# Wide weight blocks of an MLP: the last activation group transposed half a unit earlier, and one wide block made plain

## The chip, the cores and the metric

One core of a Trainium2 chip runs the whole kernel. TensorE multiplies, VectorE (DVE) and ScalarE (ACT) prepare operands and drain results, SyncE (SP) and GpSimd (POOL) issue DMAs. The metric is the device time of one execution in microseconds.

## The reference

A two-layer decoder trunk over 256 tokens of width 2048, in float32. Each layer has a mixer (a recurrent one, then attention) and an MLP with 8192 hidden features. The change is in the MLP:

```python
def squared_relu_mlp(h, w1, w2):
    return jnp.square(jax.nn.relu(h @ w1)) @ w2

h = h + squared_relu_mlp(rms_norm(h, norm_mlp[layer]), mlp_w1[layer], mlp_w2[layer])
```

## The kernel before

**Three products for one.** Each float32 operand is split into a high part (the value rounded by a cast on ACT) and a low part (what is left, a subtraction on DVE). A product is then hi x hi, lo x hi and hi x lo. In the trace the weight tiles are named `hi` and `lo`. Activations and their low parts lie side by side in `bufa` (the MLP's input) and `bufb` (the hidden features: four tiles of four feature blocks each).

**Seven products for eight.** The MLP runs in four quarters of 2048 hidden features. A quarter multiplies by w1 (2048 x 2048) and then by w2 (2048 x 2048), each as two matrices of two 512-column halves (`first`, `second`, called with n = 0 and n = 2). `blocks` (line 896) computes one such matrix. For some pairs of 128-row feature blocks it uses seven products in place of eight: two token halves, two feature blocks and two column halves make a 2 x 2 by 2 x 2 product, done with sums of the operands. Sums of activations lie in `formx` and `formh`; sums of weights are made by DVE (`s<-raw,t`, then `s<-s,raw`) and by accumulating DMAs on POOL. The units t1, a, t2, c, t3, d, t4 hold the seven products of four pairs, 12 matmuls each. The remaining rows are multiplied plainly, in units called n with 24 matmuls, 12 for each token half. A plain matrix has four n units: 7 x 12 + 4 x 24 = 180 matmuls.

**Wide blocks.** The second w1 matrix of each quarter (`wider`, line 112) uses two pairs more: two of the n units are replaced by e1 to e4 (42 matmuls for 48). Their weight sums are made from half-size pieces (`make_more`, line 228), and the activation sums that they need (`more_forms`, line 869) are made once per layer, by entries of `steps` that are run one entry per unit (line 974). The host lays out the rows of w1 for this (`by_rows`, line 1425).

**What orders the work.** `ORDERS` (line 1367) gives the order of units. Each unit fetches the weights of a unit two places ahead: SP issues the load, ACT casts to `hi`, DVE subtracts to `lo`. There are three buffers each for raw, hi and lo weights, so a cast waits until TensorE has done with the unit three places back. TensorE's order is fixed by the code, since each matmul is chained to the one before. On ACT and DVE a scheduler orders by priority, and `after` adds order without a wait. Every engine takes its instructions strictly in that order.

**Turning the hidden features.** When both token halves of a hidden column group are done, `to_h` (line 977) puts a piece of work into `later`: eight transposes by TensorE into two banks `pl`, two casts by ACT into `bufb` and two subtractions by DVE for the low parts (called the bufb lows below). `flush` runs such pieces, at the end of an n unit (line 970). In the second w1 matrix the last group but one to be turned is group 3, whose work is flushed in unit n3, just ahead of the last unit t4. Its casts come after the latest weight cast (`casts`). A later weight's low part comes after the bufb lows (`turned_h`, line 213).

Line 68 is where DVE and ACT instructions are issued, line 300 the matmuls, line 303 the transposes.

Of the kernel before, what the change touches and what calls it, by code (L numbers as in the profile page):

```python
# [41 lines left out]
def trunk_kernel(ctx, tc, head, x, xtok, xback, cols, tab, masks, pos, fin, w_in, w_gate, w_out, w_qkv, w_o, w1, w2, out):  # L42
# [66 lines left out]
    def plan(src, n):  # L109
        units.extend((src, i) for i in range(n))  # L110

    wider = lambda src, i: src is w1 and i % 16 == 8
    order_of = lambda src, i: ORDERS[3 if wider(src, i) else 0 if src is w1 and i not in (0, 64) or src is w_o and not i
                                     else 2 if src is w2 and i == 120 else 1]

# [65 lines left out]

    held = {}
    turned_h = []

    def combine(u, src, i, what, i0):
        def load(name, j, home=wraw):
            held[name] = home.tile([P, 2048], F32, name="raw" if home is wraw else "bufb2" if home is act else name)
            nc.sync.dma_start(held[name], src[j])

        def add(to, x, y):  # L190
            return V.tensor_tensor(held[to], held[x], held[y], OP.add)

        if what == "t1":
            load("t1", i, both)
            load("a", i0)
            held["s"] = both.tile([P, 2048], F32, name="s")
            i = add("s", "a", "t1")
            if src is w_qkv and i0 == 8:
                after(i, [made[u - 1].ins.name])
        elif what in ("n", "d", "e2"):  # L200
            load(what, i)
        elif what == "e1":
            load("e1", i, act)
        def make(step=2048):
            if what[0] == "e":
                make_more(u, src, what, i0)
                return
            made[u] = Weights(held[{"t1": "s", "t2": "s", "t3": "t1", "t4": "s"}.get(what, what)], step)

        if what == "n" and src is w2 and i0 % 16 == 0 and i == i0 + 6:  # L210
            make()
            for name in turned_h:
                tc.add_manual_dep(made[u].ins, name, NOSYNC, reason="order on one engine")
            return
        ahead = units[u + 1][2:3] if u + 1 < len(units) else ()
        if ahead == ("t2",):
            load("c", i0 + 5)
            nc.gpsimd.dma_start(held["t1"], src[i0 + 5], accum_op=OP.add)
            if (src is w2 and (i0 == LATE_SUM or i0 % 16 == 0)) or (src is w1 and i0 == 64):
                make()  # L220
                after(add("s", "s", "c"), [made[u].ins.name])
                return
            add("s", "s", "c")
        make()
        if what == "c":
            nc.gpsimd.dma_start(held["s"], src[i0 + 1], accum_op=OP.add)
# [80 lines left out]
    def flush(due=None):  # L307
        todo = later[:due]
        del later[:due]
        for f in todo:  # L310
            f()
# [8 lines left out]
    def after(ins, names):  # L320
        ins = getattr(ins, "ins", ins)
        for n in names:
            tc.add_manual_dep(ins, n, NOSYNC, reason="order on one engine")
        return ins.name
# [571 lines left out]
    def blocks(src, i0, n0, mov, forms, events, final):  # L896
# [47 lines left out]
        for m, (what, u) in enumerate(order):  # L944
            w = unit(src, None if u is None else i0 + 4 * n0 + u)
            due = len(later)
            if what in extra:
                for bank_, at, get in extra[what]:
                    times(bank_, w, get, at, terms=2)
            elif what == "t4" and src is w2 and i0 + 4 * n0 == 120:  # L950
                times(beta, w, side[what], 0, S, beta[:, :S])
                final(0, 1, beta)
                rest = psc.tile([P, 512], F32, name="pt", bufs=1)
                times(rest, w, side[what], S, S, rest[:, :S])
                events["rest"](rest[:, :S])
            elif what != "n":
                times(bank[what], w, side[what])
                if what == "a":
                    seed(gamma, beta)
                elif what == "t1":  # L960
                    seed(delta, alpha)
                elif what in events:
                    events[what](bank[what])
            else:
                n, g = divmod(u, 4)
                for j in range(2):
                    times(sums[n, j], w, lambda i, j=j, g=g: plain(j, 4 * g + i))
                    if ends[n, j] == m:
                        final(n, j, sums[n, j])
                flush(due)  # L970
            if what in ("c", "e2", "t4", "e4") and (what, src, i0 + 4 * n0) != ("t4", w2, 120):
                finish_sums(m)
            turn_some()
            for f in steps.pop(0) if steps else ():
                f()

    def to_h(n, tiles):
        def work():
            ps = []
            turned_h.clear()  # L980
            for y in tiles:
                ps.append(psc.tile([P, 4, P], F32, name="pl", bufs=2))
                for i in range(4):
                    turn(ps[-1][:, i], y[:, i * P:i * P + P])
            with urgent():
                for j, p in enumerate(ps):
                    b = bufb[:, 4 * n:4 * n + 4]
                    if n < 2 and j:
                        b, p = b[:, 1::2], p[:, 1::2]
                    h = b[..., j * P:j * P + P]  # L990
                    after(A.copy(h, p), casts if n == 3 else ())
                    turned_h.append(after(V.tensor_tensor(b[..., S + j * P:S + j * P + P], p, h.bitcast(F32), OP.subtract), []))
                if n < 2:
                    z = tiles[1].rearrange("p (k c) -> p k c", k=4)
                    A.copy(z, ps[1])
                    t = tiles[0].rearrange("p (k c) -> p k c", k=4)
                    (s2, s4), (a21, a22), (a11, a12) = (
                        [v.rearrange("p (m two) c -> p two m c", two=2)[:, e] for e in range(2)] for v in (t, z, ps[0]))
                    combos(a22, s2, a21, s4, a11, a21, a12, a22)
                    for v, at in ((z, slice(1, 4, 2)), (t, slice(0, 4, 2))):  # L1000
                        part_forms(formh, 2 * n, 2, at, v.rearrange("p (m two) c -> p m two c", two=2))
        later.append(work)
# [76 lines left out]
    def mlp(layer, nrm, nxt, gname):  # L1079
# [10 lines left out]
        V.tensor_scalar(r2n, r2, -1.0, None, op0=OP.mult)  # L1090
        if not gname:
            after(lut(spare, epsc, AF.Abs_reciprocal_sqrt), casts)
        steps[:] = [[] for _ in range(5)] + [[lambda: more_forms(0)], [], [lambda: more_forms(1)]]
        for q in range(4):
            ends = nxt if q == 3 else None

# [303 lines left out]
def _layout(a):  # L1400
# [27 lines left out]
        t[10], t[14] = (both[:, :, k::2].reshape(P, 4, 512) for k in range(2))  # L1428
        return t.reshape(16, P, 2048)

    w1 = np.concatenate([by_rows(toks(n(w)[:, q * 2048:q * 2048 + 2048], PAIRED)) for w in a["mlp_w1"] for q in range(4)])
    w2 = np.concatenate([toks(n(w)[q * 2048:q * 2048 + 2048], PAIRED) for w in a["mlp_w2"] for q in range(4)])
    xs = n(a["x"]).reshape(2, P, D)
    xback = xs[1, ::-1]
# [35 lines left out]
```

## Time and profile before

| | |
|---|---|
| median of 3 runs | 2108.83 us (2107.88 to 2110.83) |
| profiled execution, its own time | 2113.02 us |
| its span, first to last instruction | 2111.2 us |
| granted TensorE clock, mean | 0.999 |
| read from HBM | 506.94 MB, 241 GB/s over the span |

The span is the time between the first and the last instruction; the execution's own time holds in addition what lies before and after. Busy time of TensorE counts a matmul from its start to its modelled end, and matmuls overlap: they start every 0.227 us while one is given 0.39 us. So a start that is late by less than the overlap shows up as busy time, and lateness is read better from the distance between the starts of two places in the program. In the names of the trace `out<-in` is what an instruction writes and reads, without the numbers of buffers; `p`, `pd`, `po` and `pt` are accumulators.

### The profile page before, as it was taken

The page shows a single profiled execution, that of the slowest core. Times are in us where ns is not written, and L with a number is a line of the kernel's source. Part 1 is how long each engine was busy: PE and PEld are TensorE (multiplying, and loading weights), DVE is VectorE, ACT ScalarE, POOL GpSimd, SP SyncE. Part 2 cuts the span into 40 slices and gives each one's busy share as a digit, 9 for nine tenths or more (in the row PEclk, how much of TensorE's full clock was granted, in tenths as well). Part 3 has the DMA queues.
Part 4 walks back from the last instruction along what each step waited for, and adds up shares of the span by engine and source line. Part 5 has one row for each costly group of instructions (what it writes and reads, how often), then busy time and mean ns, then how long its engine had stood idle before and what let it go on. Part 6 is the DMA issues. An engine that isn't in the chain of part 4 may idle for free.

```text
span 2111.2 us, 24900 instructions
## 1 busy us (share of the span) xinstructions
PE 2096.7 (99%) x9652; PEld 1738.3 (82%) x9652; DVE 1769.4 (84%) x1695; ACT 1395.6 (66%) x1530; POOL 87.8 (4%) x107
## 2 busy tenths in 40 slices
PE   9999999999999999999999999999999999999998
PEld 8888888877888888888888888888888888888886
DVE  7686978988888888888988788799888887988887
ACT  7577556676576567567666777677756755765765
POOL 0000000000000000000000000000000000000000
PEclk9999999999999999999999999999999999999999
DMA  8544557878878888888888777778788789788785
GB/s 346 181 162 158 180 202 217 289 215 251 270 230 281 276 240 253 283 248 230 280 248 251 212 215 233 217 239 260 234 268 277 229 252 310 235 247 276 231 288 162
DMA packets 73047, 510.67 MB, mean 242 GB/s; under 512 B 8160, under 2 KB 8544, under 8 KB 12896
## 3 DMA queue, kind: packets, MB, share of 16 engines
q1 hardware_dynamic: 58320, 413.38, 51.8%
q0 software_dynamic: 14464, 95.43, 24.7%
q8 instruction: 76, 1.25, 0.2%
q14 instruction: 43, 0.35, 0.0%
q10 hardware_dynamic: 144, 0.26, 0.0%
HBM read 506.94 MB, written 2.10 MB: 241 GB/s over the span
## 4 chain that ended last, share of the span: by engine, by line
PE 83%; DVE 8%; issue 3%; DMA 3%; ACT 2%; SPq 0%; DVEq 0%; ACTq 0%
PE p L300 53%; PE pd L300 12%; PE po L300 11%; DVE lo L68 5%; PE pt L300 3%; ACT hi L68 2%; DMA raw<-in_w 2%; DVE s L68 2%; PE pl L303 2%; PE pl L300 2%; DVE bufb L68 1%; DMA raw<-in_w_in 1%; DVE y L68 0%; DMA both_in<-in_head 0%; DVE formx L68 0%
## 5 line engine op out<-in xcount | busy, mean ns | idle before, releaser
L68 DVE TENSOR_TENSOR lo<-raw,hi 128x2048 fp32r<-128x2048 f32 (+2 forms) x357 | 767.3, 2157 | 134.8 <-ACT hi L68 133.7
L68 ACT CAST hi<-raw 128x2048 fp32r<-128x2048 f32 (+2 forms) x357 | 641.6, 1807 | 230.9 <-PE p L300 120.6
L300 PE MATMUL p<-hi,bufa 128*128 128x512 f32 x1872 | 474.6, 393 | 0.0
L300 PEld LDWEIGHTS p<-hi,bufa 128*128 128x128 f32 x1872 | 348.1, 188 | 69.7
L68 DVE TENSOR_TENSOR lo<-s,hi 128x2048 fp32r<-128x2048 f32 x123 | 281.6, 2290 | 103.2 <-ACT hi L68 102.9
L68 ACT CAST hi<-s 128x2048 fp32r<-128x2048 f32 x123 | 235.2, 1912 | 197.8 <-DVE s L68 163.3
L300 PE MATMUL p<-hi,bufb 128*128 128x512 f32 x1240 | 310.1, 391 | 0.0
L300 PEld LDWEIGHTS p<-hi,bufb 128*128 128x128 f32 x1240 | 231.7, 188 | 48.1 <-DVE bufb L68 0.2
L300 PE MATMUL p<-lo,bufa 128*128 128x512 f32 x936 | 255.3, 390 | 0.1
L300 PEld LDWEIGHTS p<-lo,bufa 128*128 128x128 f32 x936 | 175.7, 188 | 37.7 <-DVE lo L68 1.0
L300 PE MATMUL p<-lo,bufb 128*128 128x512 f32 x620 | 169.2, 392 | 1.9 <-DVE lo L68 1.3
L300 PEld LDWEIGHTS p<-lo,bufb 128*128 128x128 f32 x620 | 115.6, 188 | 29.9 <-DVE lo L68 6.3
L68 DVE TENSOR_TENSOR s<-s,raw 128x2048 f32<-128x2048 f32 x41 | 93.8, 2287 | 6.3 <-DMA raw<-in_w_qkv 3.2
L68 DVE TENSOR_TENSOR lo<-t,hi 128x2048 fp32r<-128x2048 f32 x41 | 93.7, 2286 | 3.0 <-ACT hi L68 3.0
L68 DVE TENSOR_TENSOR s<-raw,t 128x2048 f32<-128x2048 f32 x41 | 93.8, 2287 | 0.2
L300 PE MATMUL p<-hi,formx 128*128 128x512 f32 x368 | 92.1, 392 | 0.2 <-DVE formx L68 0.2
L68 ACT CAST hi<-t 128x2048 fp32r<-128x2048 f32 x41 | 78.6, 1918 | 17.5 <-PE po L300 6.8
L300 PE MATMUL pd<-hi,bufa 128*128 128x512 f32 x352 | 88.2, 393 | 0.0
L300 PE MATMUL po<-hi,bufb 128*128 128x512 f32 (+1 forms) x352 | 88.0, 387 | 0.0
L300 PEld LDWEIGHTS p<-hi,formx 128*128 128x128 f32 x368 | 68.4, 188 | 14.8 <-DVE formx L68 0.7
L300 PE MATMUL po<-hi,bufa 128*128 128x512 f32 x296 | 77.5, 393 | 1.0 <-ACT y L68 1.0
L300 PEld LDWEIGHTS po<-hi,bufb 128*128 128x128 f32 x352 | 65.7, 188 | 13.5
(328 smaller groups left out, 2723.0 us busy)
## 6 DMA issues: line engine op xcount, KB each, us to landing
raw<-in_w SPq DMA_DIRECT2D x216, 1024.0 KB, 6.8
raw<-in_w_in SPq DMA_DIRECT2D x45, 1024.0 KB, 4.8
raw<-in_w_qkv SPq DMA_DIRECT2D x42, 1024.0 KB, 5.2
t<-in_w SPq DMA_DIRECT2D x32, 1024.0 KB, 7.7
t<-in_w POOLq DMA_DIRECT2D x32, 1024.0 KB, 9.0
s<-in_w POOLq DMA_DIRECT2D x32, 1024.0 KB, 9.3
raw<-in_w_out SPq DMA_DIRECT2D x15, 1024.0 KB, 4.8
raw<-in_w_o SPq DMA_DIRECT2D x14, 1024.0 KB, 5.1
```

The source lines that it names most:

```text
L68: i = call(*args, **kw)
L300: chain[:] = [after(T.matmul(*args, **kw), chain)]
L303: chain[:] = [after(T.transpose(out_, in_, ident), chain)]
```

## The change

1. Unit n3 of a wide block flushes the turning of group 3 after its first 12 matmuls instead of after all 24.
2. In `to_h` the casts of group 3 no longer follow the latest weight cast, and its low parts follow the latest first sum `s<-raw,t` (`first_sum`).
3. The second w1 matrix of layer 0's first quarter is no longer wide: it takes the plain order of four pairs, and its w1 rows keep the plain layout. In layer 0 `more_forms` runs 24 units into the MLP, in the first w2 matrix, instead of 5.

```diff
-    wider = lambda src, i: src is w1 and i % 16 == 8
+    wider = lambda src, i: src is w1 and i % 16 == 8 and i != 8
...
+    first_sum = []
...
             i = add("s", "a", "t1")
+            first_sum[:] = [after(i, [])]
             if src is w_qkv and i0 == 8:
...
                     if ends[n, j] == m:
                         final(n, j, sums[n, j])
+                    if not j and not n and wider(src, i0 + 4 * n0):
+                        flush(due)
+                        due = 0
                 flush(due)
...
                     h = b[..., j * P:j * P + P]
-                    after(A.copy(h, p), casts if n == 3 else ())
-                    turned_h.append(after(V.tensor_tensor(b[..., S + j * P:S + j * P + P], p, h.bitcast(F32), OP.subtract), []))
+                    A.copy(h, p)
+                    turned_h.append(after(V.tensor_tensor(b[..., S + j * P:S + j * P + P], p, h.bitcast(F32), OP.subtract), first_sum if n == 3 else []))
...
-        steps[:] = [[] for _ in range(5)] + [[lambda: more_forms(0)], [], [lambda: more_forms(1)]]
+        steps[:] = [[] for _ in range(5 if layer else 24)] + [[lambda: more_forms(0)], [], [lambda: more_forms(1)]]
...
-    w1 = np.concatenate([by_rows(toks(n(w)[:, q * 2048:q * 2048 + 2048], PAIRED)) for w in a["mlp_w1"] for q in range(4)])
+    w1 = [toks(n(w)[:, q * 2048:q * 2048 + 2048], PAIRED) for w in a["mlp_w1"] for q in range(4)]
+    w1 = np.concatenate(w1[:1] + [by_rows(w) for w in w1[1:]])
```

How this moves instructions, at three places. TensorE at the end of the wide block in layer 0's third quarter, before (unit n3 in the first four rows, the transposes of group 3, then t4):

```order
L300 MATMUL p<-hi,bufa 128x512 x8
L300 MATMUL p<-lo,bufa 128x512 x4
L300 MATMUL po<-hi,bufa 128x512 x8
L300 MATMUL po<-lo,bufa 128x512 x4
L303 MATMUL pl<-tab__188,y_6073 128x128 x4
L303 MATMUL pl<-tab__188,y_6013 128x128 x4
L300 MATMUL po<-hi,bufa 128x512 x8
L300 MATMUL po<-lo,bufa 128x512 x4
```

The same place now:

```order
L302 MATMUL p<-hi,bufa 128x512 x8
L302 MATMUL p<-lo,bufa 128x512 x4
L305 MATMUL pl<-tab__188,y_6061 128x128 x4
L305 MATMUL pl<-tab__188,y_6001 128x128 x4
L302 MATMUL po<-hi,bufa 128x512 x8
L302 MATMUL po<-lo,bufa 128x512 x4
L302 MATMUL po<-hi,bufa 128x512 x8
L302 MATMUL po<-lo,bufa 128x512 x4
```

The eight transposes stand 12 matmuls sooner. DVE at the same place, before (`s<-raw,t` is the first sum of the w2 matrix that follows, `bufb_2514<-pl` the bufb lows of group 3):

```order
L68 TENSOR_TENSOR s<-raw,t_6159 128x2048
L68 TENSOR_TENSOR lo<-s,hi 128x2048
L68 TENSOR_TENSOR bufb_2514<-pl,bufb_2514 128x4x128 x2
L68 TENSOR_TENSOR lo<-raw,hi 128x2048 x2
L68 TENSOR_TENSOR s<-s,raw 128x2048
```

DVE there now:

```order
L68 TENSOR_TENSOR s<-raw,t_6147 128x2048
L68 TENSOR_TENSOR bufb_2514<-pl,bufb_2514 128x4x128 x2
L68 TENSOR_TENSOR lo<-s,hi 128x2048
L68 TENSOR_TENSOR lo<-raw,hi 128x2048 x2
L68 TENSOR_TENSOR s<-s,raw 128x2048
```

The lows stand between the sum and its low part; the same holds in all seven wide blocks. On ACT their two casts stood behind `hi<-s` and stand ahead of it now. Last, DVE in the first w2 matrix of layer 0's first quarter as it is now (`y_4017` and `y_4060` are the two calls of `more_forms`):

```order
L68 TENSOR_TENSOR lo<-s,hi 128x2048
L68 TENSOR_TENSOR lo<-raw,hi 128x2048
L68 TENSOR_TENSOR y_4017<-bufa 128x512
L68 TENSOR_TENSOR y_4017<-y_4017 128x128 x4
L68 TENSOR_TENSOR lo<-raw,hi 128x2048
L68 TENSOR_TENSOR s<-s,raw 128x2048
L68 TENSOR_TENSOR bufa<-y_4017,bufa 128x4x128
L68 TENSOR_TENSOR y_4060<-bufa 128x512
L68 TENSOR_TENSOR y_4060<-y_4060 128x128 x2
L68 TENSOR_TENSOR lo<-s,hi 128x2048
```

Before, the two calls stood in the first w1 matrix of the quarter, among the lows of its last units, and this matrix had none of their rows.

## The prediction

> **What bounds the kernel now.** I read the page first.
>
> ```profile
> span 2111.2 us, 24900 instructions
> PE 2096.7 (99%) x9652; PEld 1738.3 (82%) x9652; DVE 1769.4 (84%) x1695; ACT 1395.6 (66%) x1530; POOL 87.8 (4%) x107
> ```
>
> TensorE is busy for 99% of the span, so only two things can change the time: the number of matmuls, and the moments at which TensorE is late. The page hardly shows the second, because matmul records overlap and a late matmul looks like a long one. So next I cut the MLP into its matrices, from the first matmul of one to the first of the next, and compared blocks that hold the same matmuls (windows view; columns: window, its length, then the busy time and count of each engine, granted clock, DMA share, GB/s).
>
> ```profile
> 442.03:483.59 41.56, 39.95 (x179) 31.42 (x177) 35.32 (x30) 28.06 (x31) 2.59 (x3) 1.00 0.68 219
> 612.27:650.77 38.50, 38.50 (x179) 32.08 (x178) 34.56 (x28) 29.71 (x33) 2.59 (x3) 1.00 0.76 237
> 483.59:527.05 43.46, 42.76 (x188) 34.50 (x189) 38.48 (x24) 26.76 (x21) 1.73 (x2) 1.00 0.86 261
> 650.77:692.77 42.00, 41.99 (x189) 34.55 (x188) 36.41 (x23) 25.22 (x19) 1.72 (x2) 1.00 0.84 262
> 816.49:859.25 42.76, 42.32 (x189) 34.48 (x188) 36.53 (x23) 25.93 (x20) 1.76 (x2) 1.00 0.83 255
> 1519.01:1562.40 43.39, 42.65 (x190) 34.44 (x189) 38.46 (x24) 26.69 (x21) 1.72 (x2) 1.00 0.86 261
> 1686.12:1728.59 42.47, 42.31 (x189) 34.40 (x188) 35.53 (x23) 25.65 (x19) 1.73 (x2) 1.00 0.82 253
> 1852.81:1894.78 41.97, 41.97 (x190) 34.54 (x188) 36.09 (x23) 24.88 (x19) 1.72 (x2) 1.00 0.84 260
> 2018.53:2061.40 42.87, 42.40 (x190) 34.41 (x188) 36.41 (x24) 26.76 (x24) 2.31 (x3) 1.00 0.88 263
> 527.05:567.85 40.80, 40.80 (x181) 33.80 (x180) 34.45 (x20) 21.92 (x14) 1.72 (x2) 1.00 0.85 276
> 1728.59:1769.89 41.30, 41.10 (x182) 33.71 (x181) 36.29 (x21) 21.94 (x14) 1.72 (x2) 1.00 0.90 284
> 567.85:609.55 41.70, 41.70 (x190) 34.62 (x188) 33.56 (x24) 27.79 (x26) 2.61 (x3) 1.00 0.86 266
> ...
> 2061.40:2076.22 14.82, 13.90 (x61) 11.19 (x60) 14.82 (x13) 10.33 (x11) 0.86 (x1) 1.00 0.81 215
> 527.05:540.65 13.60, 13.60 (x61) 11.27 (x60) 11.62 (x7) 8.67 (x7) 0.86 (x1) 1.00 0.79 222
> ```
>
> The undisturbed prices: a four-pair matrix with eight transposes costs 41.70 us (row 567.85), without transposes 40.80 (row 527.05, 180 matmuls, 0.2267 us each), and a wide block from its second unit on 38.50 (row 612.27). What stands above them is TensorE being late:
> - layer 0, first quarter: 41.56 - 38.50 = 3.06 in the wide block, 43.46 - 41.70 = 1.76 in the first w2 matrix behind it;
> - first w2 matrices of the other quarters: 0.30, 1.06 (layer 0), 1.69, 0.77, 0.27, 1.17 (layer 1);
> - later in the second w2 matrix: 0.50 in the second quarter of layer 1 (41.30 - 40.80) and 1.22 in the last (14.82 - 13.60).
>
> The fourth quarter of layer 0 has other work in its window, so I take its one late matmul, which shows 0.15 us idle, as 0.4: row 650.77 lost 0.30 with next to no idle time showing.
>
> ```profile
> 1002.37 1.19 PE L300 MATMUL p<-lo,bufb 128*128 128x512 f32 x4 [0.15 <-DVE lo L68]
> ```
>
> All of it is 12.2 us, 0.6% of the span. 4.82 lies in the quarter that loses its wide block, 7.4 behind the seven wide blocks that stay.
>
> **Why TensorE is late behind a wide block.** This is the timeline at the end of the third quarter's wide block (start, length, engine, instruction; in brackets the engine's idle time before it and its releaser).
>
> ```profile
> 809.03 0.64 ACT L68 ACTIVATE y<-y 128x512 f32<-128x512 f32 x1
> ...
> 810.16 1.98 PE L300 MATMUL po<-hi,bufa 128*128 128x512 f32 x8
> ...
> 811.47 2.30 DVE L68 TENSOR_TENSOR s<-raw,t 128x2048 f32<-128x2048 f32 x1
> ...
> 812.89 1.03 PE L303 MATMUL pl<-tab__188,y 128*128 128x128 f32 x8
> ...
> 813.80 1.91 ACT L68 CAST hi<-s 128x2048 fp32r<-128x2048 f32 x1 [2.17 <-DVE s L68]
> ...
> 815.61 1.06 ACT L68 CAST bufb<-pl 128x512 fp32r<-128x512 f32 x2
> 815.74 2.29 DVE L68 TENSOR_TENSOR lo<-s,hi 128x2048 fp32r<-128x2048 f32 x1 [1.98 <-ACT hi L68]
> ...
> 817.95 1.28 DVE L68 TENSOR_TENSOR bufb<-pl,bufb 128x512 fp32r<-128x512 f32 x2
> ...
> 819.14 4.48 DVE L68 TENSOR_TENSOR lo<-raw,hi 128x2048 fp32r<-128x2048 f32 x2
> ...
> 821.48 1.19 PE L300 MATMUL pd<-lo,bufb 128*128 128x512 f32 x4 [0.29 <-DVE lo L68]
> ```
>
> VectorE makes the sum s, then stands idle 1.98 us until ScalarE has cast it, then does lo<-s, then the two bufb lows, and only then the lo that TensorE waits for at 821.48. ScalarE idles 2.17 us before its cast.
>
> **The change, part by part.** *Transposes half a unit sooner, lows behind s.* The transposes move from 812.89 to 810.16, where their input is ready (the square ends at 809.67). The casts of their result then fall into ScalarE's 2.17 us (two take 1.06), and the bufb lows into VectorE's 1.98 us (817.95 to 819.14 is 1.19 of queue time). lo<-s keeps its start, since the cast behind s sets it; every VectorE instruction behind it comes **1.19 us sooner**. The transposes themselves are hidden by nothing and cost as before, and no DMA is issued by the moved step. Behind the lows on VectorE now stand only lo<-s and what follows, which could not start anyway; if s were late, the lows would be too, and TensorE reads them first in the third unit, two units of 12 x 0.2267 = 5.4 us after the matrix starts. The dropped order between these casts and the weights' casts costs nothing: ScalarE's idle 2.17 us hides it; without that cover the two casts would push hi<-s by their 1.06.
>
> So each of the seven quarters gains what it loses now, up to 1.19: 0.30, 1.06, 0.42 in layer 0; in layer 1 1.19, 1.19, 0.27, 1.19. The caps: 1.69 includes 0.49 at the low part of s itself, which does not move,
>
> ```profile
> 1521.27 1.20 PE L300 MATMUL p<-lo,formx 128*128 128x512 f32 x4 [0.22 <-DVE lo L68]
> ```
>
> (0.22 idle, plus the slower restart). The second quarter's 0.77 + 0.50 and the last quarter's 1.17 + 1.22 are one VectorE queue each: when TensorE is earlier by what was removed, it meets the same queue later, so both end at 1.19. Sum: **-5.6 us**. Bounds: 0 if the queue is held by something else, -7.4 if all of it goes.
>
> *The first quarter keeps four pairs.* Its four short units (42 matmuls) become two of 24: six matmuls more, 6 x 0.2267 = **+1.36 us**. The Trainium skill ("TensorE: Matmul & The Clock Gate", Back-to-back issue gap) puts sustained 512-column matmuls at about 131 ns each; by that the six would cost an estimated 0.8 us and the total gain would be 0.6 larger. The row of 180 matmuls in 40.80 us disagrees, and the row decides.
>
> What it removes is the cause of the 4.82 us:
>
> ```profile
> 414.93 1.29 DVE L68 TENSOR_TENSOR y<-bufa 128x512 f32<-128x512 f32 x2
> ...
> 419.34 0.89 DVE L68 TENSOR_TENSOR y<-y 128x128 f32<-128x128 f32 x4
> ...
> 426.37 0.69 DVE L68 TENSOR_TENSOR bufa<-y,bufa 128x512 fp32r<-128x512 f32 x1
> ...
> 426.97 0.42 DVE L68 TENSOR_TENSOR bufb<-y,bufb 128x256 fp32r<-128x256 f32 x1
> ...
> 443.19 1.23 DVE L68 TENSOR_TENSOR bufb<-bufb,raw 128x1024 f32<-128x1024 f32 x1 [3.65 <-DMA raw<-in_w]
> ...
> 447.01 1.20 PE L300 MATMUL po<-lo,bufa 128*128 128x512 f32 x4 [0.28 <-DVE lo L68]
> ...
> 464.06 0.72 PE L300 MATMUL po<-hi,bufa 128*128 128x512 f32 x2 [0.98 <-ACT y L68]
> ```
>
> At 443.19 VectorE stood 3.65 us for a load that only the wide order needs, with the lo for 447.01 queued behind; 464.06 opens a short unit that no longer exists. In place of nine half-size lows and sums at about 1.22 us stand two full lows at 2.29: 6.4 us less for VectorE, one megabyte less to load on SP's queue and two half-size accumulating loads fewer on POOL's. The rows of the weights that the host lays out otherwise are read in pieces of the same size. The extra forms (1.29 + eight at 0.22 + 0.69 + two at 0.42 = 4.6 us of VectorE) move out of w1's first half into the first w2 matrix, hidden by its free time: row 650.77 has 36.4 busy of 42.0, and VectorE arrives there with the 6.4 us in hand. I take all 4.82 as gone (bounds: 0, and 4.82); plain blocks at rows 527.05 and 567.85 lose nothing. Net **-3.46 us**.
>
> **Sum:** -5.6 - 4.82 + 1.36 = -9.1 us. The profiled execution took 2113.02 us (span 2111.2 and 1.8 around it), so it would take 2103.9. The median of the runs is 4.2 us lower, 2108.83; the same 9.1 off gives **2099.7**.
>
> **The rivals.**
> - *The extra forms collide in w2.* For: 36.4 + 4.6 = 41.0 us of VectorE in a block of 41.7, and a lo can't be made before one of three weight buffers is free, so the 6.4 us may not carry over. Against: the steps stand behind the third unit, with lows already ahead. Price: half of 4.6, so a gain of 6.8: 2102.0. 14%.
> - *Something else holds the queue behind the wide blocks* (a landing weight, DMA at 0.82 to 0.90 of its engines in these rows), and 1.19 us sooner on VectorE doesn't reach TensorE. Against: the brackets name lo, not DMA. Gain 3.5: 2105.3. 10%.
> - *The unprofiled runs hold fewer of these stalls*: they are 4.2 us shorter, and if that is stall time of the same places, 9.1 - 4.2 = 4.9 are left: 2103.9. 8%.
> - *Slower: the earlier transposes wait for their input.* At 810.16 the square is 0.49 us old. If ScalarE gets to the squares later, TensorE stands at the transposes and ScalarE's queue at the casts, ahead of hi<-s. With a margin of 0.5 in each of seven places, each us beyond it costs 7 us: from 1.8 us late it eats the gain, at 2.5 it gives -9.1 + 14 = 4.9 more, 2113.7. Against: the ScalarE instructions ahead of the squares are the same as before. 5%.
>
> That the change doesn't do what it says is excluded by the order of the instructions.
>
> **How the numbers follow.** Forecast 63%. Differences under 0.2% (4.2 us) can't be told from no change. Faster by more: forecast, first rival and half of the third, 0.81. Within: the second and half of the third, 0.14. Slower: 0.05. The range runs from 2097 (all 10.9 us of 12.2 - 1.36, and 1 us of scatter as in the three runs) to 2106.5 (past the second rival).
>
> **What would show it.** The wide block's window in the first quarter is gone and its plain one takes about 42.6 us (40.80 and two sets of transposes); the first w2 matrix behind it takes about 41.7: right if under 42.2, the first rival if above 43. In the other quarters the bufb lows stand between s and lo<-s, the bracket before lo<-s shrinks from 1.98 to about 0.7, and the first w2 matrices fall to 41.7 to 42.2, with 1519.01's keeping 0.5. The prediction is wrong if these windows keep their lengths, if TensorE waits at the transposes for y, or if a later block takes back what they gave.

## The result, and the profile after

| | median (runs) | lowest to highest | profiled execution |
|---|---|---|---|
| before | 2110.00 us (11) | 2107.88 to 2112.42 | 2113.02 us, span 2111.2 |
| changed | 2103.67 us (11) | 2103.18 to 2104.79 | 2103.96 us, span 2102.2 |

The ratio is 0.997, with a 95% interval of 0.9961 to 0.998: 6.3 us faster (4.2 to 8.2 by the interval, so the 9.1 of the forecast lies outside it). The range of the prediction, 2097.0 to 2106.5, holds the time, and the sign is right. The own time of the profiled execution came out almost on the forecast (2103.96 for 2103.9), while the median lies 4.0 us above it (2103.67 for 2099.7). The first of these is luck, as the experiments show.

First the page of the changed kernel, then its MLP matrices in the windows view, in the order of the rows of before (window, length, busy time and count of PE, PEld, DVE, ACT, POOL, then clock, DMA share, GB/s).

```profile
span 2102.2 us, 24903 instructions
PE 2091.9 (100%) x9658; PEld 1739.4 (83%) x9658; DVE 1765.5 (84%) x1688; ACT 1394.1 (66%) x1525; POOL 86.2 (4%) x105
```

```profile
438.18:480.76 42.58, 42.58 (x197) 35.45 (x196) 37.57 (x34) 31.43 (x33) 1.72 (x2) 1.00 0.81 246
480.76:522.46 41.70, 41.70 (x190) 34.62 (x189) 38.11 (x31) 24.98 (x21) 1.72 (x2) 1.00 0.81 252
646.17:687.91 41.74, 41.74 (x190) 34.57 (x188) 36.77 (x23) 24.59 (x19) 1.72 (x2) 1.00 0.88 273
811.63:853.34 41.71, 41.71 (x189) 34.57 (x188) 36.57 (x22) 24.78 (x19) 1.72 (x2) 1.00 0.87 271
977.06:1019.72 42.66, 42.66 (x198) 35.36 (x197) 38.43 (x28) 28.89 (x30) 1.73 (x2) 1.00 0.88 268
1512.12:1553.94 41.82, 41.82 (x189) 34.49 (x188) 36.98 (x22) 25.32 (x19) 1.72 (x2) 1.00 0.87 269
1677.70:1719.57 41.87, 41.87 (x190) 34.49 (x188) 37.00 (x22) 25.34 (x19) 1.75 (x2) 1.00 0.86 267
1804.78:1843.78 39.00, 38.92 (x179) 31.91 (x178) 36.25 (x32) 29.45 (x33) 2.59 (x3) 1.00 0.76 234
...
2009.38:2052.23 42.85, 42.56 (x189) 34.33 (x188) 34.56 (x22) 25.21 (x23) 2.34 (x3) 1.00 0.83 254
2052.23:2067.17 14.94, 13.92 (x61) 11.18 (x60) 14.94 (x13) 10.43 (x11) 0.86 (x1) 1.00 0.81 212
```

The first quarter's plain matrix takes 42.58 us and the w2 matrix behind it 41.70, without lateness. Six of the seven first w2 matrices behind wide blocks have come down to their undisturbed length within 0.2 us. The last one (42.85 where it was 42.87) and what follows it (14.94 where it was 14.82) have not moved at all.

The transition that the prediction showed at 809 to 821, now in the changed kernel (timeline; the third quarter of layer 0):

```profile
805.30 1.03 PE L305 MATMUL pl<-tab__188,y 128*128 128x128 f32 x8
...
805.99 0.58 ACT L68 CAST bufb<-pl 128x512 fp32r<-128x512 f32 x1
...
806.99 0.59 ACT L68 CAST bufb<-pl 128x512 fp32r<-128x512 f32 x1
808.46 1.91 ACT L68 CAST hi<-s 128x2048 fp32r<-128x2048 f32 x1 [0.88 <-DVE s L68]
...
806.15 2.28 DVE L68 TENSOR_TENSOR s<-raw,t 128x2048 f32<-128x2048 f32 x1
808.35 1.28 DVE L68 TENSOR_TENSOR bufb<-pl,bufb 128x512 fp32r<-128x512 f32 x2
810.41 2.29 DVE L68 TENSOR_TENSOR lo<-s,hi 128x2048 fp32r<-128x2048 f32 x1 [0.78 <-ACT hi L68]
812.62 4.49 DVE L68 TENSOR_TENSOR lo<-raw,hi 128x2048 fp32r<-128x2048 f32 x2
```

The bracket ahead of lo<-s fell from 1.98 to 0.78 us, ScalarE's ahead of hi<-s from 2.17 to 0.88: the casts and the low parts fill what had been waiting, and the next two low parts follow lo<-s at once. From the start of s to the low part behind lo<-s it is now 6.47 us (806.15 to 812.62), and it was 7.67 (811.47 to 819.14): 1.20 sooner, where the prediction said 1.19. The transposes do not wait for y.

**Where the 9.06 us between the two profiled executions lie** (starts of the same matrices in both): 1.14 ahead of the MLP, before anything that the change touches; 3.45 in the first quarter; 4.50 in the seven first w2 matrices; 0.49 in the second w2 matrix of layer 1's second quarter; given back are 0.49 in one wide block (39.00 in place of 38.51) and 0.12 in the last matrix; the rest is under 0.1. So the change itself is worth 7.9 us in this pair, not 9.06.

### The profile page after: what moved, and what is told of

Read it like the earlier page. It is cut to its first block, busy times and chain, and to the rows that moved or that the text cites. A ratio compares the mean times of both kernels' runs of the same rounds, so it can differ in the third digit from the quotient of the medians.

```text
span 2102.2 us, 24903 instructions
## 1 busy us (share of the span) xinstructions
PE 2091.9 (100%) x9658; PEld 1739.4 (83%) x9658; DVE 1765.5 (84%) x1688; ACT 1394.1 (66%) x1525; POOL 86.2 (4%) x105
## 4 chain that ended last, share of the span: by engine, by line
PE 96%; DVE 1%; DMA 1%; issue 1%; ACT 0%; DVEq 0%; ACTq 0%
PE p L302 60%; PE po L302 15%; PE pd L302 14%; PE pt L302 3%; PE pl L305 2%; PE pl L302 2%; DMA raw<-in_w 1%; DVE lo L68 1%; DVE s L68 0%; ACT hi L68 0%; PE po L368 0%; PE po L305 0%; DVE xall L68 0%; DVE formx L68 0%; PE pd L305 0%
## 5 line engine op out<-in xcount | busy, mean ns | idle before, releaser
L302 PEld LDWEIGHTS pd<-hi,bufa 128*128 128x128 f32 x352 | 65.3, 188 | 13.1
```

Of the source, the lines that this page charges most:

```text
L302: chain[:] = [after(T.matmul(*args, **kw), chain)]
```

## The experiments

Twelve runs follow: ten kernels with an edit, and the kernel before twice more. Each time of before that is named beside a kernel is from the same set of runs as that kernel. The changed kernel was not timed again in these sets, so a difference from its 2103.67 us also holds what differs between them: before took 2110.00 us beside the changed kernel, and 2110.06, 2110.21, 2110.55 and 2110.99 beside the others.

**The two edits apart.** The first quarter alone, with the turning of before:

```diff
-                    if not j and not n and wider(src, i0 + 4 * n0):
-                        flush(due)
-                        due = 0
...
-                    A.copy(h, p)
-                    turned_h.append(after(V.tensor_tensor(...), first_sum if n == 3 else []))
+                    after(A.copy(h, p), casts if n == 3 else ())
+                    turned_h.append(after(V.tensor_tensor(...), []))
```

> Only the first edit: layer 0's first quarter keeps four pairs and gets its forms later; the seven other wide blocks turn their last group as before. My theory (the terms of the prediction are separate and add up): the first quarter alone gives its net -3.5 us, in the trace as a second w1 matrix of 42.6 us and a first w2 matrix of 41.7 us, and the seven wide transitions keep the lateness that the profile of before shows (7.4 us in all, each within some tenths of its value there). Rival A (the stalls differ between executions): the seven transitions sum to clearly less or more than 7.4 us in this execution, by over 1.5 us, although their code is that of before; then the time against before lies nearer to -2 us. Rival B (the four pairs only pay together with the new turning): nothing, within 1 us.

And the turning alone, all eight blocks wide, with the forms at step 5:

```diff
-    wider = lambda src, i: src is w1 and i % 16 == 8 and i != 8
+    wider = lambda src, i: src is w1 and i % 16 == 8
...
-        steps[:] = [[] for _ in range(5 if layer else 24)] + ...
+        steps[:] = [[] for _ in range(5)] + ...
```

> Only the second edit: all eight wide blocks turn their last group half a unit sooner, with the low parts behind the next first sum; the first quarter stays wide with its forms early. My theory: the seven later blocks give 3 to 5.6 us as in the changed kernel's trace (first w2 matrices of 41.7 to 41.9 us, the last quarter's still near 42.9), and the first quarter keeps the 3.1 us of its wide block, while its first w2 matrix falls from 43.5 by up to 1.2 us. In all -4 to -6 us. Rival (the stalls differ between executions, before's profiled one was rich in them): -2 to -3 us.

Measured, before at 2110.06 (33 runs, 2107.21 to 2112.66): the first quarter alone 2108.18 (2106.32 to 2110.15), ratio 0.9992 [0.9983, 1.0], so 1.9 us (0 to 3.6 by the interval); the turning alone 2105.19 (2104.36 to 2105.88), 0.9979 [0.997, 0.9988], so 4.9. Together 6.8, the whole change 6.3: they add up nearly. (The turning alone also took 1.06 us from the first quarter's w2 matrix, 42.40 where it was 43.46, which the four pairs take as well; so the two should exceed the whole by about 1.) But the first quarter gives 1.9 where its trace shows 3.45. Which transitions are late in its trace, with the code of before there, also differs from before's. That is what rival A said, though the seven differ in sum by 1.1 us and not by the 1.5 that it named:

```profile
978.28:1022.41 44.13, 43.22 (x197) 35.32 (x196) 39.64 (x30) 29.70 (x30) 1.73 (x2) 1.00 0.87 259
1514.80:1557.53 42.73, 42.31 (x189) 34.47 (x188) 37.78 (x24) 26.05 (x20) 1.73 (x2) 1.00 0.84 262
1681.43:1724.37 42.94, 42.43 (x190) 34.40 (x189) 38.07 (x24) 26.24 (x20) 1.75 (x2) 1.00 0.84 261
```

These are the fourth quarter of layer 0 (undisturbed 42.66), and the first two of layer 1: 1.47, 1.03 and 1.24 us late, where before's profile has 0.9, 1.69 and 0.77. The turning alone leaves the first quarter late: its wide block is 41.11 us long, and the matrix behind it is 0.70 late (42.40).

**The kernel before, profiled twice more.** No edit.

> The kernel before, profiled once more, to see which of its stalls are of the code and which of one execution. Theory (the profiled execution of before was rich in stalls: 2113.0 us, where the median of 44 timed runs is 2110): the first quarter's 4.8 us and the seven wide transitions' 7.4 us come out smaller in most executions, by about 3 us together, with the same places but other sizes (the kernel with the first quarter alone, whose seven transitions have before's code, had 5.1 there). Rival (the stalls are of the code alone and the 3 us lie elsewhere, in start-up or attention): first quarter and transitions repeat within 0.5 us each.

> The same kernel a second time, with the same expectations: 9 to 10 us for the two sums together by the first theory, 12.2 by the rival.

They took 2109.67 and 2112.89 us. One window over everything from the first wide unit to the last w2 matrix, of before as first profiled, of these two, and of the changed kernel, one row each:

```profile
396.73:2076.22 1679.49, 1673.59 (x7601) 1382.04 (x7600) 1437.08 (x1140) 1123.18 (x1120) 84.34 (x99) 1.00 0.81 251
```

```profile
396.07:2072.88 1676.81, 1672.23 (x7602) 1382.17 (x7600) 1436.90 (x1140) 1124.18 (x1120) 84.52 (x99) 1.00 0.81 251
```

```profile
395.92:2076.03 1680.11, 1674.42 (x7602) 1381.44 (x7600) 1436.84 (x1140) 1123.45 (x1120) 84.53 (x99) 1.00 0.81 251
```

```profile
395.59:2067.17 1671.58, 1669.88 (x7607) 1383.86 (x7606) 1433.44 (x1133) 1121.86 (x1115) 82.66 (x97) 1.00 0.82 252
```

The same program needs 1676.8 to 1680.1 us for it; against 1671.6 the change is worth 7.9, 5.2 or 8.5 us, according to which execution of before one takes. By place, the first w2 matrices behind the wide blocks (length in us, from the windows of each execution; the sum is of what lies above 41.70, or 42.65 in the fourth quarter of layer 0):

| kernel | l0 q2 | l0 q3 | l0 q4 | l1 q1 | l1 q2 | l1 q3 | l1 q4 | sum late |
|---|---|---|---|---|---|---|---|---|
| before | 42.00 | 42.76 | 43.57 | 43.39 | 42.47 | 41.97 | 42.87 | 6.2 |
| before, second execution | 42.04 | 42.13 | 42.86 | 42.75 | 42.87 | 41.98 | 42.80 | 4.6 |
| before, third execution | 42.29 | 42.28 | 43.12 | 43.03 | 42.48 | 43.05 | 43.04 | 6.4 |
| first quarter alone | 41.90 | 41.99 | 44.13 | 42.73 | 42.94 | 42.23 | 42.03 | 5.1 |
| turning alone | 41.74 | 41.70 | 42.64 | 41.76 | 41.70 | 41.71 | 42.79 | 1.2 |
| changed | 41.74 | 41.71 | 42.66 | 41.82 | 41.87 | 41.88 | 42.85 | 1.7 |

The first quarter repeats better: its wide block was 41.56, 40.99 and 40.95 us, the matrix behind it 43.46, 43.47 and 43.45. So neither theory holds whole: the transitions scatter by 2 us in sum, the first quarter by 0.6, and the third execution was no milder than the first.

What scatters is the lead with which VectorE starts the first sum `s<-raw,t` ahead of the w2 matrix. In the three executions of before it is 4.35 to 5.77 us (outside layer 0's fourth quarter, which has other work), and each of these eighteen matrices is late by 6.05 us less that lead, to within 0.1: the third quarter of layer 0, for one, has a lead of 5.02 (811.47 to 816.49) and is 1.06 late. The new turning needs 1.2 us less, about 4.85, and the changed kernel's leads there are 4.79 to 5.88. Why the lead scatters stays open.

What follows is the size of the error: a single execution of before can't give the change's worth to better than about 3 us, while the changed kernel, which has lost six of the seven scattering places, keeps within 1.6 us over its 11 runs.

**The two halves of the new turning.** Only the transposes early, casts and low parts in their old places:

```diff
-                    A.copy(h, p)
-                    turned_h.append(after(V.tensor_tensor(...), first_sum if n == 3 else []))
+                    after(A.copy(h, p), casts if n == 3 else ())
+                    turned_h.append(after(V.tensor_tensor(...), []))
```

> The changed kernel, but only TensorE's transposes come half a unit sooner: ScalarE's two casts of them stay behind its cast for the next form, and VectorE's low parts stay behind the next low part, as before. My theory (what counts is the place in VectorE's queue, 1.2 us per low part): the first w2 matrices behind the seven wide blocks are as late as before's, 42.0 to 43.4 us, and the time lies 3 to 5.6 us above the changed kernel, near the kernel with the first quarter alone. Rival (the late transposes themselves were the cause): most of the gain stays, first w2 matrices at 41.7 to 41.9 us, within 1 us of the changed kernel.

Casts and low parts in their new places, the transposes late:

```diff
-                    if not j and not n and wider(src, i0 + 4 * n0):
-                        flush(due)
-                        due = 0
```

> The changed kernel, but its transposes stand where they stood before, half a unit later; ScalarE's casts and VectorE's low parts keep their new places. My theory (the new places are only worth what the earlier transposes give them): ScalarE's casts now wait at the head of its queue for the late transposes and hold the cast for the next form some 1 us, so the first w2 matrices are as late as before's or up to 1 us later: 3 to 10 us above the changed kernel. Rival (the order of the queues alone is the gain): within 1 us of the changed kernel.

Measured: 2108.05 us (2106.71 to 2110.04), 0.9992 [0.9983, 1.0001], with early transposes alone, 4.4 above the changed kernel and level with the first quarter alone (2108.18). Moving the transposes by itself gains nothing: in its profiled execution, the slowest of its eleven runs, the seven matrices are 6.9 us late in sum. The timeline, in layer 1's third quarter, is that of before: lo<-s waits its 1.98 us and the bufb lows stand behind it.

```profile
1847.80 2.29 DVE L68 TENSOR_TENSOR lo<-s,hi 128x2048 fp32r<-128x2048 f32 x1 [1.98 <-ACT hi L68]
1850.01 1.28 DVE L68 TENSOR_TENSOR bufb<-pl,bufb 128x512 fp32r<-128x512 f32 x2
```

With the order alone 2107.47 us (2106.50 to 2108.70), 0.9988 [0.9979, 0.9998], 3.8 above. The lower end of the 3 to 10 came out, by the wait that was expected (same place):

```profile
1843.40 1.07 ACT L68 CAST bufb<-pl 128x512 fp32r<-128x512 f32 x2 [1.90 <-PE pl L305]
1844.36 1.92 ACT L68 CAST hi<-s 128x2048 fp32r<-128x2048 f32 x1
...
1846.31 2.29 DVE L68 TENSOR_TENSOR lo<-s,hi 128x2048 fp32r<-128x2048 f32 x1 [1.01 <-ACT hi L68]
...
1848.66 1.20 PE L302 MATMUL p<-lo,formx 128*128 128x512 f32 x4 [0.21 <-DVE lo L68]
```

ScalarE's casts wait 1.90 us at the head of its queue for the transposes, hi<-s goes behind them, and TensorE waits for lo<-s instead. That loss is no longer a matter of chance: the seven matrices are 0.6 to 0.75 us late, every one (42.31, 42.33, 43.39, 42.35, 42.31, 42.31, 42.38), 4.5 us in sum. On top of the first quarter each half alone gives 0.1 and 0.7 us, both together 4.5 (2108.18 to 2103.67).

**The forms as early as before**, in the changed kernel:

```diff
-        steps[:] = [[] for _ in range(5 if layer else 24)] + ...
+        steps[:] = [[] for _ in range(5)] + ...
```

> The changed kernel, but layer 0's forms are made as early as before (step 5 instead of 24), although its first quarter needs them no sooner. Theory of the prediction (VectorE's queue carries the first quarter's lateness, and the forms' small instructions stand in it between low parts): TensorE is late again in the first quarter, by 1 to 3 us over its second w1 and first w2 matrix (42.6 and 41.7 us in the changed kernel), and the time rises by as much. Rival (the wide layout with its fewer matmuls alone was too fast for VectorE, the four pairs give it room enough for the forms as well): the two windows and the time stay within 0.4 us of the changed kernel.

2105.00 us (2104.82 to 2105.71), 1.3 above the changed kernel. TensorE loses it in one place:

```profile
441.06 2.29 DVE L68 TENSOR_TENSOR s<-s,raw 128x2048 f32<-128x2048 f32 x1 [4.09 <-DMA raw<-in_w]
...
443.72 0.62 ACT L68 CAST formh<-y 128x512 fp32r<-128x512 f32 x1 [3.49 <-DVE y L68]
...
445.40 2.11 PE L302 MATMUL p<-hi,bufa 128*128 128x512 f32 x8 [1.27 <-ACT p L68]
```

VectorE stands 4.09 us at the head of its queue for a load, ScalarE stands behind it for y, and the copy of p that TensorE needs stands behind that. With the forms in the queue, and a sum put ahead of it, the low part that frees the load's buffer ends later, at 431.0 instead of 427.2; the load then goes out 1.7 us behind one of GpSimd's (429.34), where it went 2.7 ahead of it, and takes twice as long. The rows are the issues from 427 to 428 in the changed kernel, and from 431 to 432 with early forms (last column: us to landing).

```profile
raw<-in_w SPq DMA_DIRECT2D x1, 1024.0 KB, 4.8
```

```profile
raw<-in_w SPq DMA_DIRECT2D x1, 1024.0 KB, 9.9
```

The w2 matrix behind it takes 41.69 us with early forms too. So both parts of the first edit count: of the first quarter's 4.8 us (4.2 to 4.3 in the other two executions of before) the forms' place is worth 1.3, and the rest goes with the four pairs.

**Why the last quarter did not move.** In the changed kernel ScalarE's cast of the second weight behind the late sum waits for a landing, and the late low parts come from there:

```profile
2035.64 1.91 ACT L68 CAST hi<-raw 128x2048 fp32r<-128x2048 f32 x1 [7.84 <-DMA raw<-in_w]
...
2039.94 1.20 PE L302 MATMUL p<-lo,bufb 128*128 128x512 f32 x4 [0.22 <-DVE lo L68]
...
2060.67 1.20 PE L302 MATMUL p<-lo,bufb 128*128 128x512 f32 x4 [1.02 <-DVE lo L68]
```

That quarter alone loads four rows of final gains (y<-in_fin, 256 KB each, one row broadcast to 128 partitions) on GpSimd's queue. Issues of before (2030.5 to 2035), then of the changed kernel (2021 to 2024); last column: us to landing.

```profile
s<-in_w POOLq DMA_DIRECT2D x1, 1024.0 KB, 9.3
raw<-in_w SPq DMA_DIRECT2D x1, 1024.0 KB, 10.1
y<-in_fin POOLq DMA_DIRECT2D x1, 256.0 KB, 3.3
```

```profile
s<-in_w POOLq DMA_DIRECT2D x1, 1024.0 KB, 12.8
raw<-in_w SPq DMA_DIRECT2D x1, 1024.0 KB, 12.1
y<-in_fin POOLq DMA_DIRECT2D x1, 256.0 KB, 5.3
```

And when they were issued, in the timeline of both:

```profile
2031.31 0.56 POOL L1085 DMA_DIRECT2D y<-in_fin  x1 [13.33 <-PE pl L303]
2032.54 0.88 POOL L226 DMA_DIRECT2D s<-in_w  x1 [0.68 <-DVE lo L68]
2034.47 0.33 SPq L188 DMA_DIRECT2D raw<-in_w  x1
```

```profile
2021.42 0.56 POOL L1090 DMA_DIRECT2D y<-in_fin  x1 [13.95 <-PE pl L305]
2021.97 0.92 POOL L228 DMA_DIRECT2D s<-in_w  x1
2023.49 0.33 SPq L189 DMA_DIRECT2D raw<-in_w  x1
```

Counted from the start of the matrix (2018.53, 2009.38), the change issues the raw load 1.83 us sooner (15.94, now 14.11). It lands no sooner (15.94 + 10.1, now 14.11 + 12.1), and s now follows the row of gains by 0.55 us instead of 1.23. The theory is that the loads run into each other. The first test moves three of the four rows behind GpSimd's next load of weights:

```diff
+            i = after(nc.gpsimd.dma_start(held["t1"], src[i0 + 5], accum_op=OP.add), [])
+            if src is w2 and i0 == 120:
+                for f in late:
+                    f(i)
...
+            gain_row(1)
+            late.append(lambda i: [gain_row(n, [i]) for n in (0, 2, 3)])
```

> The changed kernel, but three of the four rows of final gains that it loads at the start of the last w2 pair (256 KB each, broadcast from one row to 128 partitions, on GpSimd's queue ahead of the weights) are issued some 45 us later, behind that queue's next weight load. Theory (in the last quarter the low parts wait for weights that land late because these rows share the transfer engines: the first raw tile lands 26.2 us into that matrix, in the third quarter 24.9): the last quarter's first w2 matrix falls from 42.85 to 41.8 to 42.3 us and the 1.2 us behind it shrinks by some tenths; 0.5 to 1.2 us below the changed kernel. Rival (VectorE's own work there, two multiplications by the gains and the late sum, sets it): 42.85 stays within 0.2 us, and the time within 0.3 us.

2101.46 us (2101.22 to 2102.85), 0.9955 [0.9943, 0.9968] against before (2110.99 here). Its windows:

```profile
2009.77:2051.46 41.69, 41.69 (x190) 34.58 (x188) 36.84 (x24) 26.06 (x23) 3.39 (x5) 1.00 0.85 265
2051.46:2065.06 13.60, 13.60 (x62) 11.27 (x60) 13.43 (x11) 9.87 (x11) 0.91 (x1) 1.00 0.89 272
```

Both stretches are undisturbed, a gain of 2.5 us in the trace and 2.2 in the median, more than expected: the 1.2 us in the last matrix went as well. In this trace the one row that stays goes out at 2004.98, 4.8 us ahead of the matrix, so no row stands ahead of s. The s load took 9.2 us and the raw load 8.6.

The next kernel moves all four rows there and, besides, VectorE's four multiplications by the first two of them behind its last low part:

```diff
-                        turns.append([-3, gain])
+                        held_gains.append(gain)
...
+        for f in held_gains:
+            f(last_low)
```

> As the kernel with three rows late, but all four rows go behind that weight load, and the four multiplications of VectorE by the first two of them (0.6 us each, now in the queue ahead of low parts that TensorE waits for) go behind the last low part, where VectorE idles 3.6 us. Theory (strict queue order: each multiplication ahead of a late low part costs TensorE its length): a further 0.6 to 1.2 us, the wait of 1.18 us in the last w2 matrix goes; 1.2 to 2.3 us below the changed kernel in all. Rival (the late landing alone counts): the same as with three rows late, within 0.3 us. Rival (the end of the kernel becomes longer, as VectorE is late for the last scaling): above it.

2101.74 us (2101.09 to 2102.13), 0.9955 [0.9942, 0.9969], no more than with three rows late: VectorE's multiplications had room, and the first rival holds. Where the rows stand, by two further kernels. One adds the loads to layer 1's third quarter as well, where nothing reads them:

```diff
-                second(..., gains if ends and not gname and not n else None)
+                second(..., gains if q > 1 and not gname and not n else None)
```

> The changed kernel with four more loads of the rows of final gains, 256 KB each, in layer 1's third quarter at the place where the last quarter has them; nothing reads them, and VectorE gets no multiplication there. Theory (those loads make the weights behind them land late): the third quarter's first w2 matrix rises from 41.9 to 42.4 to 42.9 us, with its second raw load behind the late sum at 11 to 12 us from issue to landing where it was 9.6. Rival (something else of the last quarter does it): 41.7 to 42.0 us.

That quarter's matrix took 41.71 us (one execution, 2104.40), and its raw load 9.9: the theory failed there. But there the fourth row went out 0.6 us into the matrix and not 12 us, so it never stood just ahead of s; only rows that go out that early are shown to be harmless. The other kernel keeps four pairs in the last quarter (it is named after_again here, but is no repeat of the changed kernel):

```diff
-    wider = lambda src, i: src is w1 and i % 16 == 8 and i != 8
+    wider = lambda src, i: src is w1 and i % 16 == 8 and i not in (8, 120)
...
-    w1 = np.concatenate(w1[:1] + [by_rows(w) for w in w1[1:]])
+    w1 = np.concatenate(w1[:1] + [by_rows(w) for w in w1[1:7]] + w1[7:])
```

> The changed kernel, but the last quarter keeps four pairs as well, with its loads of gains where they are. Theory (TensorE loses about 2.4 us in the last quarter because weights land late there, and six more matmuls, 1.36 us, only push that landing's deadline back by as much or nothing): 0.5 to 1.4 us above to 1.0 us below the changed kernel; its last quarter's first w2 matrix at 42.3 to 42.9 us. Rival (the wide block's speed is the cause): first w2 matrix 41.7 us and 13.6 us behind it, 1.1 us below the changed kernel, still above the kernel with the rows of gains late.

2103.05 us (2102.84 to 2105.09), 0.9967 [0.9955, 0.9979], with 41.69 and 13.60 us in the two windows: by the times the rival. It isn't clean, though. In this kernel the order on GpSimd's queue changed by itself, s at 2021.84 and the row behind it at 2023.12, and the loads took

```profile
s<-in_w POOLq DMA_DIRECT2D x1, 1024.0 KB, 8.8
raw<-in_w SPq DMA_DIRECT2D x1, 1024.0 KB, 10.0
y<-in_fin POOLq DMA_DIRECT2D x1, 256.0 KB, 10.4
```

Of the 3.6 us by which the raw load landed sooner in its matrix, 1.5 are that it was issued sooner (12.58 us into the matrix instead of 14.11), and 2.1 are the load itself. So the last kernel puts this one row behind s in the changed kernel and leaves the other three:

```diff
+            late_sum[:] = [after(nc.gpsimd.dma_start(held["s"], src[i0 + 1], accum_op=OP.add), [])]
...
-                nc.gpsimd.dma_start(fing[n], ...)
+                after(nc.gpsimd.dma_start(fing[n], ...), late_sum if n == 1 else [])
```

> The changed kernel, but one of its four loads of the rows of final gains, the one that GpSimd's queue has 0.55 us ahead of the accumulating load for the last w2 pair's late sum, stands right behind that load; the other three stay where they are. Theory (this one load directly ahead is what slows the late sum's load to 12.8 us and the raw load behind it to 12.1): those take 8.8 to 9.3 and 8.6 to 10.1 us, the raw tile lands 22.6 to 23.3 us into the matrix instead of 26.2, the matrix lasts 41.7 us and what follows 13.6 instead of 14.9; 2.0 to 2.5 us below the changed kernel, as with three rows late. Rival (all four rows share the blame): the raw tile lands at 24 to 25.5 us and the gain is 0.5 to 1.5 us.

2103.11 us (2100.52 to 2103.49; 0.9962 [0.9948, 0.9975]), and in its profiled execution

```profile
2009.66:2051.40 41.74, 41.74 (x189) 34.50 (x188) 34.22 (x22) 24.97 (x23) 2.29 (x3) 1.00 0.84 263
2051.40:2066.33 14.93, 13.90 (x61) 11.19 (x60) 14.93 (x13) 10.44 (x11) 0.87 (x1) 1.00 0.80 212
```

s took 9.4 us, about as expected, but the raw load issued 1.4 us behind the row took 11.3 and landed 25.1 us into the matrix. That is what the rival named (24 to 25.5 us, and a gain of 0.5 to 1.5; the median is 0.6 below the changed kernel, or 1.1 if each is taken against its own before). The first stretch is cured and the second is not. Two of its five runs are at 2100.5 and 2101.0, three at 2103.1 to 2103.5; only one of the three was profiled, and how the five fall apart is left open.

All fourteen profiled executions side by side say more than each test alone. The table has the distance from the issue of the row to that of s, what s and the raw load took, when the raw load had landed (its cast starts then; in us from the start of the matrix), and what TensorE lost over both stretches (their lengths above 41.70 and 13.60).

| executions | row ahead of s by | s took | raw took | raw landed | lost |
|---|---|---|---|---|---|
| changed; early forms; rows in the third quarter too | 0.54 to 0.55 | 12.3 to 12.9 | 12.1 to 12.5 | 26.3 to 26.4 | 2.5 to 2.6 |
| order alone; turning alone | 0.72; 0.76 | 10.5; 11.1 | 10.4; 11.3 | 25.8; 26.2 | 2.0; 2.4 |
| first quarter alone | 0.96 | 9.7 | 10.4 | 25.5 | 1.7 |
| before (three times); early transposes alone | 1.23 to 1.28 | 9.3 to 9.8 | 9.9 to 10.2 | 26.0 to 26.4 | 2.2 to 2.6 |
| row behind s by 0.55 | none | 9.4 | 11.3 | 25.2 | 1.4 |
| four pairs; row behind s by 1.28 | none | 8.8 | 10.0 | 22.7 | 0.0 |
| three or four rows late | none | 9.2 | 8.6 | 22.9; 22.8 | 0.0 |

The loss is the landing less 23.8 us in every one of them, to within 0.1, and nothing where the landing is sooner. So the raw load's landing sets what the last quarter loses, in before as well: there 1.17 of the 2.39 showed at the transition, and when the new turning removed that, TensorE came to the same landing that much sooner and waited for it. And on the whole s takes the longer the closer the row stands ahead of it.

## Why the prediction was right, and where it was not

- **What bounds the kernel** (TensorE's lateness, read from matrices of the same matmuls): right. Blocks without lateness repeat within 0.05 us across all kernels, and the change's gains were found in the places named, but for the last quarter.
- **Six matmuls for 1.36 us:** right; the plain matrix takes 42.58 us, the forecast said 42.6.
- **The first quarter, net 3.46:** right in the profile of before on which it was worked out (3.45). The second and third execution of before had 0.6 us less to remove there. The cause given, VectorE's queue behind a load and the forms in it, is shown for the forms (1.3 us when they go back); that the four pairs remove the rest is shown by the difference alone.
- **1.19 us for each of seven wide blocks:** the mechanism is right and both of its halves are needed, as the two half-kernels show. Six places became undisturbed to within 0.2 us. The cap did not hold in the first quarter of layer 1, which gained 1.57: the 0.49 us at lo<-s, said not to move, went too. That is no work of the change: s started 4.35 us ahead of the matrix in the profile of before and 4.83 in that of the changed kernel, 0.48 sooner. In layer 0's fourth quarter I had put 0.42 where the windows of both kernels differ by 0.91.
- **The last quarter's 1.19:** wrong, it gave nothing. The step that failed is "one VectorE queue": I took it as the cause from the bracket that names lo. Behind the lo stood a landing, as my second rival had it (price 3.5 for all seven places; it held in one). The raw load went out 1.83 us sooner and landed no sooner, some 26.2 us into the matrix as before, and that landing sets the 2.4 us of both stretches.
- **The sum:** 9.1 was forecast, 9.06 is the difference of the profiles, and that is luck: the missing 1.2 us of the last quarter were made up by 1.14 us ahead of the MLP, which no part of the change reaches, and smaller misses cancel.
- **The step to the median** is what put the forecast 4.0 us off. "The median of the runs is 4.2 us lower, 2108.83; the same 9.1 off gives" took the stalls of one execution for those of all. The third rival (fewer stalls in the other runs) was the better account: timed, the change gives 6.3 and not 9.1. That accounts for 2.8 of the 4.0; the other 1.2 is that three runs of before gave 2108.83 and eleven gave 2110.00. The rival's own 2103.9 is nearly the measured median, by a larger stall deficit (4.2) against a lower start, so that agreement is luck too.
- **The extra forms in w2** and **the transposes waiting for y:** neither came. The w2 matrix with the forms took 41.70 us with 38.11 of VectorE in it. The 0.49 us that one wide block took longer (39.00), most of it where TensorE waits for y in a short unit, is no cost of the change: the third execution of before has 38.95 in that same block.

The Trainium skill ("DMA: Bandwidth & Descriptors", Anatomy of one DMA — SWDGE (gpsimd) path) fits a load on GpSimd's queue by 2.0 us and its bytes at 436 GB/s, an estimated 2.6 us for 256 KB and 4.4 for a megabyte. The rows above disagree, with 3.3 to 10.4 and 8.8 to 12.8 us beside other loads; the measured ones decide.

The version with three rows of gains late, on top of the change, beats both kernels: 2101.46 us against 2103.67 for the changed one, and their runs do not overlap (2101.22 to 2102.85; 2103.18 to 2104.79). The two were timed apart; each against its own before, they are 9.5 and 6.3 us faster.

## What to carry to other kernels

Price a change from more than one execution when what it removes are stalls: the undisturbed blocks repeat to 0.05 us, the stalls don't, so take a block's undisturbed length from the trace and its lateness from several executions. Set the lateness beside the start or the landing that it may hang on, over all executions at hand: here both kinds of stall, which seemed to scatter, followed one line each. In a queue that runs strictly in order, an instruction whose input is late belongs behind those that TensorE waits for, and one whose input is early into the wait; the input has to be made early too, or the wait only changes its place. When a bracket names a compute engine, follow that engine's own wait one step further: behind it may stand a landing that no earlier issue brings forward.

## What the runs showed of the hardware

A megabyte on SP's queue that was issued 2.7 us ahead of the next load landed in 4.8 us; issued 1.7 us behind an accumulating megabyte on GpSimd's queue the same load took 9.9. In the last quarter such a load took 8.6 us beside one accumulating load, and up to 12.5 with a 256 KB broadcast row as well.

A broadcast row of 256 KB cost the loads near it far more than its bytes. The accumulating load s took 12.3 to 12.9 us when issued 0.54 to 0.55 us behind it (three executions), 10.5 and 11.1 at 0.72 and 0.76, 9.3 to 9.8 from 0.96 to 1.28 us on, and 9.2 with no row ahead. The raw load behind both took 12.1 to 12.5 us at the closest and 8.6 without the row, so a quarter of a megabyte cost 3.5 us or more.
